# Gates of two branches by seven block products ahead of attention, and low halves of weight blocks on POOL

## The chip, the cores and the metric

The kernel runs on one core of a Trainium2 chip, as one launch. The metric is the device time in microseconds (us), from runs without the profiler; a profile comes from one execution more, and its span runs from the first to the last instruction. The engines are named as in the profile: PE (TensorE, matmuls), PEld (its weight loads), DVE (VectorE), ACT (ScalarE), POOL (GpSimd) and SP (SyncE, which issues the DMAs here).

## The reference

Two layers work on x, 512 tokens of 1024 channels, in float32. Three token mixers take their inputs from one projection of x; each is projected to 1024 channels, weighted by a sigmoid gate of its own, summed, and projected once more. A gated FFN of width 2816 follows.

```python
for l in range(DEPTH):
    proj = jnp.einsum('bsd,de->bse', x, w_in[l])
    (na_q, na_k, na_v, df_q, df_k, df_v, m_cq, m_ckv, m_kr, gate_pre) = jnp.split(proj, split_points, axis=-1)
    na_out = neighbourhood_attention(...)   # 8 heads of 64
    df_out = diff_attention(...)            # 4 heads, two softmaxes each
    mla_out = latent_attention(...)         # 8 heads, low-rank q and kv
    gates = jax.nn.sigmoid((gate_pre + b_gate[l]).astype(jnp.float32)).astype(x.dtype)
    gates = gates.reshape(b, s, N_BRANCH, D_MODEL)
    merged = (gates[:, :, 0] * jnp.einsum('bse,ed->bsd', na_out, w_branch[l, 0])
              + gates[:, :, 1] * jnp.einsum('bse,ed->bsd', df_out, w_branch[l, 1])
              + gates[:, :, 2] * jnp.einsum('bse,ed->bsd', mla_out, w_branch[l, 2]))
    mix = jnp.einsum('bsd,de->bse', merged, w_out[l])
    x = layer_norm(DN_ALPHA * x + mix, ln1_g[l], ln1_b[l])
    gu = jnp.einsum('bsd,df->bsf', x, w_ffn_in[l])
    hidden = jax.nn.silu(gu[..., :D_FF]) * gu[..., D_FF:]
    x = layer_norm(DN_ALPHA * x + jnp.einsum('bsf,fd->bsd', hidden, w_ffn_out[l]), ln2_g[l], ln2_b[l])
```

In differential attention a head's two probability matrices are combined, multiplied with the values, normalised by their root mean square, and scaled.

## The kernel before

**Float32 by halves.** Each float32 operand is split into a high half (a copy by ACT into the type fp32r) and a low half (the difference, by DVE). A product is three matmuls (`mm3`): high by high, high by low, low by high. x is held transposed as `xth` and `xtl`, channels on the partitions. Weights come by DMA in blocks of 128x1024 into `raw` (two buffers) and are split by `wsplit` into `whi` and `wlo` (four buffers each, lines 138 and 139).

**A layer.** First `na_values` projects the values of neighbourhood attention, token tile by token tile, while the layer norm of the layer before still delivers x. `latents` projects the low-rank inputs of latent attention in two column halves of 336. Then come four pairs of neighbourhood heads, four pairs of latent heads and four heads of differential attention, a last list, the output projection, and the FFN.

**Filler.** Attention's chains (scores, maximum, exponential, transposes, split, values) leave gaps on PE. `PLAN` is a table of thirteen lists: what is emitted after each of the four pairs, four pairs and four heads, and at the end. `G20h` means the gate of branch 2 for the first 256 of its 1024 columns (the second digit counts these steps): eight k tiles, two column blocks of 128, 48 matmuls of 512 tokens, then a Tanh (line 672); "h" says where the result lies. `M20` is the merge: a projection of a branch by `w_branch`, gated and added. Branch 0 is neighbourhood, 1 differential, 2 latent attention. Gates depend only on x and the weights, so they can stand anywhere after x; merges need their branch's attention, and those of branch 1 all four heads of the differential attention (though their first k tiles need only the first heads). A scheduler with a timeline of its own orders each engine's instructions when the kernel is built, by their emission and priorities; on the chip each engine runs its list in that order and waits where an operand is missing.

**A differential head** is `df_proj` (projection, rotation, transposes of q and k, their halves; the low half of k is copied to the other 64 partitions by DMA, in `stacks_k`), then `df_head` with four passes, one for each 128 queries: two score banks (lines 476, 477), two maxima (478) and exponentials (479), reciprocal, factor and combination (481 to 483), four transposes (486), the split `PP` (221, 222), four pairs of value matmuls (491, 492), and the scaling and normalisation of the result (494, 495, 497, POOL's 231 and 232, 499). After four passes the result is transposed (503) and split with a scale (224, 225).

**Seven block products.** In the FFN all but the first two sets of columns use `ffn_fast`: two weight column blocks (gate and up) by two halves of the tokens would be eight block products of 512 channels; with sums of weight blocks and sums of x (`x_sums`, formed once per layer after the second set, 26 DVE operations) seven do. Each `product` is 24 matmuls of 256 tokens (line 784).

Of the kernel before, what the change touches and what calls it, by code (L numbers as in the profile page):

```python
# [9 lines left out]
F32 = mybir.dt.float32  # L10
# [25 lines left out]
PLAN = [i.split() for i in (  # L36
    "G20h",
    "",
# [6 lines left out]
    "G03h M03",  # L45
    "",
    "M20 G21g G22h M21 M22",
# [29 lines left out]
def f32(ap):  # L77
    return ap.bitcast(F32)
# [3 lines left out]
def trunk(ctx, tc, x, ln_in, w_in, feat, bias, lamv, w_mla, w_mlr, w_mlv, w_branch, w_out,  # L82
# [22 lines left out]
    expo = cp.tile([128, 2], F32, name="expo")  # L105
    xd = [xs.tile([128, D], F32, name=f"xd{t}") for t in range(NT)]

    def bank(tag):
# [13 lines left out]

    def wload(segs, nk, ncol, now=True):
        raw = wp.tile([128, 1024], F32, tag="raw", name="raw", bufs=2)
        rv = raw[:, :nk * ncol].rearrange("p (k c) -> p k c", k=nk)
        c = 0
        for src in segs:
            w = src.shape[1]
            nc.sync.dma_start(rv[:, :, c:c + w], src.rearrange("(k p) c -> p k c", p=128))
            c += w  # L130
        hi, lo = wsplit(raw, nk * ncol, now)
        return hi.rearrange("p (k c) -> p k c", k=nk), lo.rearrange("p (k c) -> p k c", k=nk)

    def wsplit(raw, n, now=True):
        hi = wp.tile([128, 1024], F32R, tag="whi", name="whi")
        lo = wp.tile([128, 1024], F32R, tag="wlo", name="wlo")
        with tc.high_priority() if now else ExitStack():
            A.activation(hi[:, :n], raw[:, :n], AF.Copy)  # L138
            V.tensor_sub(lo[:, :n], raw[:, :n], f32(hi[:, :n]))  # L139
        return hi[:, :n], lo[:, :n]  # L140
# [5 lines left out]

    def wload_ks(src_of, widths, steps, now=True):

        res, k = [], 0
        for n in steps:  # L150
            res.append((k, n, wload(src_of(k * 128, (k + n) * 128), n, widths, now)))
            k += n
        return res
# [201 lines left out]
    def na_pair(l, p, vals):  # L355
        src = lambda a, b: [w_in[l, a:b, C_NQ + p * 128:C_NQ + (p + 1) * 128],
                            w_in[l, a:b, C_NK + p * 128:C_NK + (p + 1) * 128]]
        ch = wload_ks(src, 256, (4, 4))
        pq, pk = bank("acc"), bank("acc")
# [72 lines left out]
    def df_values(l, g):  # L432

        c = slice(C_DV + g * 256, C_DV + (g + 1) * 256)
        ch = wload_ks(lambda a, b: [w_in[l, a:b, c]], 256, (4, 4))
        vals = []
        for t in range(NT):
            p = bank("acc")[:, :256]
            gemm_x(p, ch, slice(0, 256), XT, tsl(t), KD)
            v = R.get()  # L440
            vv = v.rearrange("p (h s d) -> p h s d", h=2, s=2)
            split(vv[:, :, 0], vv[:, :, 1], p.rearrange("p (h d) -> p h d", h=2))
            vals.append(v)
        return vals

    def df_proj(l, h):
        src = lambda a, b: [w_in[l, a:b, C_DQ + h * 128:C_DQ + (h + 1) * 128],
                            w_in[l, a:b, C_DK + h * 128:C_DK + (h + 1) * 128]]
        ch = wload_ks(src, 256, (4, 4))
        stg = H.get()  # L450
# [57 lines left out]

    def latents(l, g):
        lat = [H.get() for _ in range(NT)]  # L510
        krs = [i[:, 672:800] for i in lat]
        for i in krs:
            G.memset(i, 0.0)
        for hf in range(2):
# [3 lines left out]
            for t in range(NT):  # L518
                p = bank("acc")[:, :336]
                gemm_x(p, ch, slice(0, 336), XT, tsl(t), KD)  # L520
                A.activation(lat[t][:, hf * 336:(hf + 1) * 336], p, AF.Copy)
        for t in range(NT):
            for a, b in ((0, 384), (384, 640)):
# [140 lines left out]
    def gates(l, b, mp, bg, dst):  # L664

        gc = C_GATE + b * D + mp * 256
        ch = wload_ks(lambda a, e: [w_in[l, a:e, gc:gc + 256]], 256, (4, 4))
        for mi in range(2):
# [5 lines left out]
    def merge(l, b, mp, o, merged, gt, first, mg=None):  # L674

        act = tuple(KTiles([t[i] for t in o]) for i in range(2))
        ch = wload_ks(lambda a, e: [w_branch[l, b, a:e, mp * 256:(mp + 1) * 256]], 256, (4,))
        for mi in range(2):
# [143 lines left out]

    def ffn_fast(l, m, sums):


        def load(t, base, kh):
            c = slice(base + m * 128, base + (m + 2) * 128)
            nc.sync.dma_start(t.rearrange("p (k c) -> p k c", k=4),
                              w_ffn_in[l, kh * 512:(kh + 1) * 512, c].rearrange("(k p) c -> p k c", p=128))
            return t  # L830
# [3 lines left out]

        g0, u0, u1 = load(H.get(), 0, 0), load(H.get(), D_FF, 0), load(H.get(), D_FF, 1)
        s = H.get()
        g1 = load(wp.tile([128, 1024], F32, tag="raw", name="raw", bufs=2), 0, 1)
        px, py, pz = bank("sc"), bank("pv"), bank("sc")
        product(px, halved(g0), from_x(0, 0), True)
        p1 = ptile()  # L840
        A.activation(p1, px, AF.Copy)
        t1, t2, t3, t4 = sums
        with tc.high_priority():
# [18 lines left out]
        H.put(s, u0, g0, u1)  # L862
        res = [hidden(px, p1)]
        res.append(hidden(u2, u3))
        return res

# [23 lines left out]
    for l in range(DEPTH):  # L890
# [18 lines left out]
        vals = na_values(l, na_v, na_slots)  # L909
        tiles, cq, ckv, kr = latents(l, fp[:, 25:30])  # L910
        merged, held, outs = [], {}, [[], [], []]
        mg = [[], []]

        def fill(steps):

            for kind, b, mp, *place in steps:
                b, mp, place = int(b), int(mp), "".join(place)
                if kind == "G":
# [10 lines left out]
                    if b:  # L929
                        held[b, mp] = pool, slot, gt  # L930
                    gates(l, b, mp, bg, gt)
                elif b == 0:
# [164 lines left out]
```

## Time and profile before

| what | value |
|---|---|
| time, median of 3 runs | 1848.38 us (1847.4 to 1851.75) |
| time of the profiled execution | 1850.09 us |
| its span | 1847.0 us |
| PE busy | 1814.9 us, 11248 matmuls |
| DVE busy | 1309.9 us, 2204 instructions |
| ACT busy | 897.8 us, 1612 instructions |
| POOL busy | 90.1 us, 165 instructions |
| mean granted clock of PE | 0.998 |

A row of the timeline gives start and duration in us, engine, line, operation, output and inputs, partitions x elements; what stands in brackets is the idle time before it and what ended it. A row of the table of groups gives the count, the total busy time and the mean in ns of one, then the idle time before. A row of the table by stretches gives for each stretch of the span the busy time and the number of instructions of each engine, the granted clock of PE, and the share and rate of the DMA engines. Matmuls overlap in PE's pipeline: what one costs is the distance between the starts of two, not its duration.

### The profile page before, as it was taken

The page shows a single profiled execution, that of the slowest core. Times are in us where ns is not written, and L with a number is a line of the kernel's source. Part 1 is how long each engine was busy: PE and PEld are TensorE (multiplying, and loading weights), DVE is VectorE, ACT ScalarE, POOL GpSimd, SP SyncE. Part 2 cuts the span into 40 slices and gives each one's busy share as a digit, 9 for nine tenths or more (in the row PEclk, how much of TensorE's full clock was granted, in tenths as well). Part 3 has the DMA queues.
Part 4 walks back from the last instruction along what each step waited for, and adds up shares of the span by engine and source line. Part 5 has one row for each costly group of instructions (what it writes and reads, how often), then busy time and mean ns, then how long its engine had stood idle before and what let it go on. Part 6 is the DMA issues. An engine that isn't in the chain of part 4 may idle for free.

```text
span 1847.0 us, 28601 instructions
## 1 busy us (share of the span) xinstructions
PE 1814.9 (98%) x11248; PEld 1617.9 (88%) x11248; DVE 1309.9 (71%) x2204; ACT 897.8 (49%) x1612; POOL 90.1 (5%) x165
## 2 busy tenths in 40 slices
PE   7999999999999999999999999999999999999997
PEld 5988899988888999999789888999888799899996
DVE  6488887665568767777756888867655687676766
ACT  4567776555433433334336677755554234333331
POOL 4100000000001000000001000000000000000001
PEclk9999999999999999999999999999999999999999
DMA  7453232222262132323445332322233512323222
GB/s 258 116 164 95 89 94 75 83 78 86 85 201 81 58 114 81 117 89 103 151 123 170 112 98 87 92 63 87 75 98 103 182 58 94 113 92 108 93 98 80
DMA packets 167766, 195.86 MB, mean 106 GB/s; under 512 B 8529, under 2 KB 132689, under 8 KB 167633
## 3 DMA queue, kind: packets, MB, share of 16 engines
q1 hardware_dynamic: 167632, 194.05, 33.7%
q8 instruction: 88, 1.44, 0.3%
q14 instruction: 46, 0.37, 0.1%
HBM read 177.24 MB, written 9.44 MB: 101 GB/s over the span
## 4 chain that ended last, share of the span: by engine, by line
PE 89%; DVE 5%; DMA 3%; ACT 1%; issue 1%; SPq 0%; POOLq 0%; DVEq 0%; POOL 0%; ACTq 0%
PE acc L157 18%; PE acc L158 18%; PE acc L156 17%; PE sc L784 9%; PE pv L784 7%; DVE wlo L139 2%; PE tr L648 2%; PE sc L156 1%; DMA f<-in_w_ffn_in_dram 1%; PE sc L158 1%; PE sc L157 1%; PE pv L157 1%; PE pv L158 1%; PE pv L156 1%; PE pv L491 1%
## 5 line engine op out<-in xcount | busy, mean ns | idle before, releaser
L138 ACT ACTIVATE whi<-raw 128x1024 fp32r<-128x1024 f32 (+3 forms) x246 | 254.3, 1034 | 289.4 <-PE acc L157 54.1
L139 DVE TENSOR_TENSOR wlo<-raw,whi 128x1024 fp32r<-128x1024 f32 (+3 forms) x246 | 293.6, 1195 | 132.2 <-ACT whi L138 129.0
L156 PE MATMUL acc<-xth,whi 128*128 128x512 f32 x512 | 204.0, 399 | 0.3 <-ACT f L672 0.3
L158 PE MATMUL acc<-xth,wlo 128*128 128x512 f32 x512 | 202.7, 396 | 0.0
L157 PE MATMUL acc<-xtl,whi 128*128 128x512 f32 x512 | 202.6, 396 | 0.0
L138 ACT ACTIVATE whi<-f 128x1024 fp32r<-128x1024 f32 x90 | 94.6, 1057 | 182.4 <-PE acc L158 102.3
L157 PE MATMUL acc<-wlo,r 128*128 128x512 f32 (+1 forms) x440 | 171.3, 390 | 2.2 <-DVE wlo L139 2.2
L158 PE MATMUL acc<-whi,r 128*128 128x512 f32 (+1 forms) x440 | 170.7, 389 | 0.0
L156 PE MATMUL acc<-whi,r 128*128 128x512 f32 (+1 forms) x440 | 169.0, 390 | 0.6 <-ACT whi L138 0.5
L157 PE MATMUL acc<-wlo,xth 128*128 128x256 f32 (+2 forms) x544 | 162.4, 299 | 1.3 <-DVE wlo L139 1.3
L156 PE MATMUL acc<-whi,xth 128*128 128x256 f32 (+2 forms) x544 | 161.7, 299 | 1.7 <-ACT whi L138 1.6
L158 PE MATMUL acc<-whi,xtl 128*128 128x256 f32 (+2 forms) x544 | 162.2, 299 | 0.0
L784 PE MATMUL pv<-r,whi 128*128 128x256 f32 x864 | 156.0, 280 | 2.3 <-DVE P L853 2.0
L784 PEld LDWEIGHTS pv<-r,whi 128*128 128x128 f32 x864 | 132.3, 188 | 5.2 <-issue 2.8
L139 DVE TENSOR_TENSOR wlo<-f,whi 128x1024 fp32r<-128x1024 f32 x90 | 109.4, 1221 | 34.7 <-ACT whi L138 34.7
L784 PE MATMUL sc<-xth,whi 128*128 128x256 f32 x432 | 120.5, 279 | 0.0
L784 PE MATMUL pv<-r,wlo 128*128 128x256 f32 x432 | 120.5, 279 | 0.0
L784 PE MATMUL sc<-xtl,whi 128*128 128x256 f32 x432 | 120.3, 279 | 0.0
L784 PE MATMUL sc<-xth,wlo 128*128 128x256 f32 x432 | 119.9, 279 | 0.0
L156 PEld LDWEIGHTS acc<-xth,whi 128*128 128x128 f32 x512 | 96.3, 188 | 19.5 <-ACT f L672 0.7
L157 PEld LDWEIGHTS acc<-xtl,whi 128*128 128x128 f32 x512 | 96.4, 188 | 18.8
L158 PEld LDWEIGHTS acc<-xth,wlo 128*128 128x128 f32 x512 | 96.4, 188 | 18.7
(255 smaller groups left out, 4462.2 us busy)
## 6 DMA issues: line engine op xcount, KB each, us to landing
raw<-in_w_in_dram SPq DMA_DIRECT2D x64, 512.0 KB, 3.7
f<-in_w_ffn_in_dram SPq DMA_DIRECT2D x54, 512.0 KB, 3.7
raw<-in_w_ffn_out_dram SPq DMA_DIRECT2D x44, 512.0 KB, 3.7
raw<-in_w_ffn_in_dram SPq DMA_DIRECT2D x34, 512.0 KB, 3.5
raw<-in_w_in_dram SPq DMA_DIRECT2D x64, 256.0 KB, 3.3
raw<-in_w_branch_dram SPq DMA_DIRECT2D x24, 512.0 KB, 3.3
raw<-in_w_out_dram SPq DMA_DIRECT2D x16, 512.0 KB, 3.6
r<-r SPq DMA_DIRECT2D x56, 128.0 KB, 2.7
```

The lines of the kernel that those rows point to most:

```text
L138: A.activation(hi[:, :n], raw[:, :n], AF.Copy)
L139: V.tensor_sub(lo[:, :n], raw[:, :n], f32(hi[:, :n]))
L156: T.matmul(o, lh[0], rh[0], start=first, stop=False)
L157: T.matmul(o, lh[0], rh[1], start=False, stop=False)
L158: T.matmul(o, lh[1], rh[0], start=False, stop=last)
L491: T.matmul(po[:, 0:256], ch_[:, tsl(k)], v, start=k == 0, stop=False)
L648: T.transpose(pt[:, tsl(i)], prs[i % 2][:, tsl(kp + i // 2)], ident)
L784: T.matmul(o[:, c], w[a][:, j, f], x[e], start=fresh and mi == 0 and j == 0 and n == 0, stop=j == 3 and n == 2, skip_group_check=True)
```

## The change

Two parts. The gates of branches 1 and 2 (eight steps of 256 columns per layer) are no longer formed by plain products as filler. `gates_fast` forms two steps at once by the seven block products that the FFN had; their code is now `block_set`, used by both. A layer has four such sets, and they are emitted around the two halves of the latents (two for branch 2 ahead of and between the halves, two for branch 1 behind them), all behind `x_sums`, which is now formed in attention too. Their Tanh runs on quarters of 256 tokens, and the results are stored to DRAM tiles `gd`; where `PLAN` has the G step of branch 1 or 2, only a load from there is left. `G20h` is moved from the first list to the tenth.

The second part: in attention's plain blocks (`na_pair`, `df_values`, `df_proj`, the gates of branch 0 and the merges, 40 blocks per layer) the low half is formed on POOL, in two operations of 512 columns, in place of one of 1024 on DVE.

```diff
@@ PLAN
-    "G20h",
+    "",
@@
-    "",
+    "G20h",
     "M20 G21g G22h M21 M22",
@@ trunk
+    gd = {(b, mp): xs.tile([128, 1024], F32, name=f"gd{b}{mp}") for b in (1, 2) for mp in range(4)}
@@ wsplit
         with tc.high_priority() if now else ExitStack():
             A.activation(hi[:, :n], raw[:, :n], AF.Copy)
-            V.tensor_sub(lo[:, :n], raw[:, :n], f32(hi[:, :n]))
+            if pool:
+                for a in range(0, n, 512):
+                    c = slice(a, min(a + 512, n))
+                    G.tensor_tensor(lo[:, c], raw[:, c], f32(hi[:, c]), op=OP.subtract)
+            else:
+                V.tensor_sub(lo[:, :n], raw[:, :n], f32(hi[:, :n]))
@@ na_pair, df_values, df_proj, gates, merge
-        ch = wload_ks(src, 256, (4, 4))
+        ch = wload_ks(src, 256, (4, 4), pool=True)
@@ latents
-    def latents(l, g):
+    def latent_rows(l, between):
         lat = [H.get() for _ in range(NT)]
-        krs = [i[:, 672:800] for i in lat]
-        for i in krs:
-            G.memset(i, 0.0)
+        between(0)
         for hf in range(2):
...
                 A.activation(lat[t][:, hf * 336:(hf + 1) * 336], p, AF.Copy)
+            between(1 + hf)
+        between(3)
+        return lat
@@ ffn_fast
-    def ffn_fast(l, m, sums):
+    def block_set(wsrc, top, bottom, sums):
...
-        res = [hidden(px, p1)]
-        res.append(hidden(u2, u3))
-        return res
+        return (px, p1), (u2, u3)
+
+    def ffn_fast(l, m, sums):
+        return [hidden(*i) for i in block_set(w_ffn_in[l], m * 128, D_FF + m * 128, sums)]
+
+    def gates_fast(l, b, mp, bg, sums):
+
+        col = C_GATE + b * D + mp * 256
+        for th, blocks in enumerate(block_set(w_in[l], col, col + 256, sums)):
+            for i, blk in enumerate(blocks):
+                t = ptile() if th == 0 and i == 0 else blk
+                for mi in range(2):
+                    m = b * 8 + 2 * (mp + i) + mi
+                    c = slice(mi * 256, mi * 256 + 256)
+                    A.activation(t[:, c], blk[:, c], AF.Tanh, bias=bg[:, m:m + 1], scale=0.5)
+                dst = gd[b, mp + i].rearrange("p (m t) -> p m t", m=2)
+                nc.sync.dma_start(dst[:, :, th * 256:th * 256 + 256], t.rearrange("p (m t) -> p m t", m=2))
@@ layer
-        tiles, cq, ckv, kr = latents(l, fp[:, 25:30])
+        sums = x_sums()
+        lat = latent_rows(l, lambda i: gates_fast(l, 2 - i // 2, i % 2 * 2, bg, sums))
...
+        tiles, cq, ckv, kr = latents(l, fp[:, 25:30], lat)
@@ fill
-                    gates(l, b, mp, bg, gt)
+                        for i in range(2):
+                            nc.sync.dma_start(gt[i], gd[b, mp][:, i * 512:(i + 1) * 512])
+                    else:
+                        gates(l, b, mp, bg, gt)
```

Before, PE's rows in the last head of differential attention of layer 0 mix the head's score, transpose (`tr`) and value (`pv`) matmuls with gate matmuls (`acc`, from `xth`):

```order
L476 MATMUL sc<-r_82,r_101 128x512
L477 MATMUL sc<-r_83,r_101 128x512
L156 MATMUL acc<-xth,whi 128x512
L491 MATMUL pv<-r_92,PP 128x256
L157 MATMUL acc<-xtl,whi 128x512
L158 MATMUL acc<-xth,wlo 128x512
L486 MATMUL tr<-cons,P 128x128 x3
L492 MATMUL pv<-r_92,PP 128x128
```

In the changed kernel the same head has on PE, from its third pass's scores on (482 and 483 are now the scores, 492 the transposes, 497 and 498 the values):

```order
L482 MATMUL sc<-r_82,r_89 128x512
L483 MATMUL sc<-r_83,r_89 128x512
L482 MATMUL sc<-r_98,r_88 128x512
L483 MATMUL sc<-r_99,r_88 128x512
L492 MATMUL tr<-cons,P 128x128 x4
L497 MATMUL pv<-r_108,PP 128x256
L498 MATMUL pv<-r_108,PP 128x128
L497 MATMUL pv<-r_109,PP 128x256
```

The gate matmuls between the head's own rows are gone. The place ahead of it, between head 2's last value matmul and head 3's first scores, reads on PE after the change (465 and 468 transpose q and k of head 3, 509 the result of head 2, `acc` is a merge's part):

```order
L498 MATMUL pv<-r_101,PP 128x128
L465 MATMUL tr<-cons,f_112 128x128 x4
L509 MATMUL tr<-cons,ost 128x128 x2
L468 MATMUL tr<-cons,f_112 128x128 x4
L162 MATMUL acc<-r_92,whi 128x512 x2
L163 MATMUL acc<-r_93,whi 128x512
L164 MATMUL acc<-r_92,wlo 128x512
L163 MATMUL acc<-r_93,whi 128x512
L164 MATMUL acc<-r_92,wlo 128x512
L482 MATMUL sc<-r_98,r_88 128x512
```

Ten transposes and six merge matmuls stand there, and the keys' transposes (468) stand behind the result's (509). At the start of layer 0, DVE had between the split of the values (`r` from `acc`) and the low halves of the latents' weights:

```order
L222 TENSOR_TENSOR r_78<-acc,r_78 128x2x128
L222 TENSOR_TENSOR r_79<-acc,r_79 128x2x128
L139 TENSOR_TENSOR wlo<-raw,whi 128x1008 x2
L222 TENSOR_TENSOR r_80<-acc,r_80 128x2x128
L139 TENSOR_TENSOR wlo<-raw,whi 128x672
```

and has after the change, in part (766 to 778 are `x_sums`, 857 to 859 sums of weight blocks, 145 a low half):

```order
L228 TENSOR_TENSOR r_89<-gt,r_88 128x512
L857 TENSOR_TENSOR f_117<-f_115,f_116 128x1024
L774 TENSOR_TENSOR xs<-xs,xtl 128x512
L777 TENSOR_TENSOR gt<-gt,xtl 128x512
L145 TENSOR_TENSOR wlo<-f_114,whi 128x1024
L228 TENSOR_TENSOR r_79<-acc,r_79 128x2x128
L766 TENSOR_TENSOR gt<-xth 128x512
L858 TENSOR_TENSOR f_115<-f_114,f_115 128x1024
L228 TENSOR_TENSOR r_93<-xs,r_92 128x512
L228 TENSOR_TENSOR r_80<-acc,r_80 128x2x128
L228 TENSOR_TENSOR r_95<-gt,r_94 128x512
L859 TENSOR_TENSOR f_114<-f_117,f_114 128x1024
```

The sums of x and of the first set's weights now stand among the values' splits, ahead of the latents' low halves.

More of the change, by code (lines that the diff above doesn't have):

```diff
@@ L120, in ptile, with wload @@
         return dp.tile([128, 512], F32, tag="P", name="P", bufs=4)
-    def wload(segs, nk, ncol, now=True):
+    def wload(segs, nk, ncol, now=True, pool=False):
         raw = wp.tile([128, 1024], F32, tag="raw", name="raw", bufs=2)
@@ L130, in wload, with wsplit @@
             c += w
-        hi, lo = wsplit(raw, nk * ncol, now)
+        hi, lo = wsplit(raw, nk * ncol, now, pool)
         return hi.rearrange("p (k c) -> p k c", k=nk), lo.rearrange("p (k c) -> p k c", k=nk)
-    def wsplit(raw, n, now=True):
+    def wsplit(raw, n, now=True, pool=False):
         hi = wp.tile([128, 1024], F32R, tag="whi", name="whi")
@@ L145, in wload_flat, with wload_ks @@
         return wsplit(raw, n)
-    def wload_ks(src_of, widths, steps, now=True):
+    def wload_ks(src_of, widths, steps, now=True, pool=False):
         res, k = [], 0
         for n in steps:
-            res.append((k, n, wload(src_of(k * 128, (k + n) * 128), n, widths, now)))
+            res.append((k, n, wload(src_of(k * 128, (k + n) * 128), n, widths, now, pool)))
             k += n
@@ L434, in df_values @@
         c = slice(C_DV + g * 256, C_DV + (g + 1) * 256)
-        ch = wload_ks(lambda a, b: [w_in[l, a:b, c]], 256, (4, 4))
+        ch = wload_ks(lambda a, b: [w_in[l, a:b, c]], 256, (4, 4), pool=True)
         vals = []
@@ L448, in df_proj @@
                             w_in[l, a:b, C_DK + h * 128:C_DK + (h + 1) * 128]]
-        ch = wload_ks(src, 256, (4, 4))
+        ch = wload_ks(src, 256, (4, 4), pool=True)
         stg = H.get()
@@ L521, in latents @@
                 A.activation(lat[t][:, hf * 336:(hf + 1) * 336], p, AF.Copy)
+            between(1 + hf)
+        between(3)
+        return lat
+    def latents(l, g, lat):
+        krs = [i[:, 672:800] for i in lat]
+        for i in krs:
+            G.memset(i, 0.0)
         for t in range(NT):
@@ L666, in gates @@
         gc = C_GATE + b * D + mp * 256
-        ch = wload_ks(lambda a, e: [w_in[l, a:e, gc:gc + 256]], 256, (4, 4))
+        ch = wload_ks(lambda a, e: [w_in[l, a:e, gc:gc + 256]], 256, (4, 4), pool=True)
         for mi in range(2):
@@ L676, in merge @@
         act = tuple(KTiles([t[i] for t in o]) for i in range(2))
-        ch = wload_ks(lambda a, e: [w_branch[l, b, a:e, mp * 256:(mp + 1) * 256]], 256, (4,))
+        ch = wload_ks(lambda a, e: [w_branch[l, b, a:e, mp * 256:(mp + 1) * 256]], 256, (4,), pool=True)
         for mi in range(2):
@@ L821, in ffn_plain, with load @@
         return res
-    def ffn_fast(l, m, sums):
-        def load(t, base, kh):
-            c = slice(base + m * 128, base + (m + 2) * 128)
+    def block_set(wsrc, top, bottom, sums):
+        t1, t2, t3, t4 = sums
+        def load(t, col, kh):
             nc.sync.dma_start(t.rearrange("p (k c) -> p k c", k=4),
-                              w_ffn_in[l, kh * 512:(kh + 1) * 512, c].rearrange("(k p) c -> p k c", p=128))
+                              wsrc[kh * 512:(kh + 1) * 512, col:col + 256].rearrange("(k p) c -> p k c", p=128))
             return t
@@ L833, in halved @@
             return wsplit(t, 1024)
-        g0, u0, u1 = load(H.get(), 0, 0), load(H.get(), D_FF, 0), load(H.get(), D_FF, 1)
+        g0, u0, u1 = load(H.get(), top, 0), load(H.get(), bottom, 0), load(H.get(), bottom, 1)
         s = H.get()
-        g1 = load(wp.tile([128, 1024], F32, tag="raw", name="raw", bufs=2), 0, 1)
+        g1 = load(wp.tile([128, 1024], F32, tag="raw", name="raw", bufs=2), top, 1)
         px, py, pz = bank("sc"), bank("pv"), bank("sc")
@@ L841, in ffn_fast @@
         A.activation(p1, px, AF.Copy)
-        t1, t2, t3, t4 = sums
         with tc.high_priority():
@@ L909, in trunk @@
         vals = na_values(l, na_v, na_slots)
-        tiles, cq, ckv, kr = latents(l, fp[:, 25:30])
+        sums = x_sums()
+        lat = latent_rows(l, lambda i: gates_fast(l, 2 - i // 2, i % 2 * 2, bg, sums))
+        for t in sums:
+            for hl in t:
+                R.put(*hl)
+        tiles, cq, ckv, kr = latents(l, fp[:, 25:30], lat)
         merged, held, outs = [], {}, [[], [], []]
```

## The prediction

> **What bounds the kernel now.** I read the page's busy times and chain first, then the table by stretches of 25 us, then the timeline of single stages.
>
> ```profile
> span 1847.0 us, 28601 instructions
> ...
> PE 1814.9 (98%) x11248; PEld 1617.9 (88%) x11248; DVE 1309.9 (71%) x2204; ACT 897.8 (49%) x1612; POOL 90.1 (5%) x165
> ...
> PE 89%; DVE 5%; DMA 3%; ACT 1%; issue 1%; SPq 0%; POOLq 0%; DVEq 0%; POOL 0%; ACTq 0%
> ```
>
> TensorE (PE) is busy nearly throughout, and 89% of the chain that ends last is its own matmuls. Only 32.1 us of the span (1847.0 - 1814.9) lie idle on it. So time can be won only by fewer matmul columns, and can be lost wherever PE begins to wait. VectorE (DVE) comes second, and the table by stretches shows where it is close behind:
>
> ```profile
> core 0: us, PE busy (x) PEld busy (x) DVE busy (x) ACT busy (x) POOL busy (x), PEclk, DMA share, GB/s
> ...
> 25.00:50.00 25.00, 24.40 (x126) 20.44 (x125) 11.63 (x17) 9.29 (x17) 5.08 (x4) 1.00 0.74 217
> ...
> 450.00:475.00 25.00, 25.00 (x119) 20.60 (x118) 15.82 (x26) 13.24 (x24) 0.00 (x0) 1.00 0.32 96
> 1300.00:1325.00 25.00, 25.00 (x120) 20.74 (x119) 15.21 (x23) 12.81 (x22) 1.58 (x4) 1.00 0.37 103
> ...
> 725.00:750.00 25.00, 24.53 (x209) 24.36 (x208) 22.44 (x25) 11.65 (x14) 0.00 (x0) 1.00 0.38 125
> ```
>
> 25 to 50 is the values' projection and the latents. 450 to 475 and 1300 to 1325 are the last heads of differential attention in layers 0 and 1: PE never waits there, because gate matmuls stand between the heads' own rows. 725 to 750 is a block set of the FFN with the sums of x: DVE is at 22.44 of 25, and PE just begins to wait. The changed kernel takes the filler out of the first kind of stretch and puts block sets where the values are.
>
> **What the block products save.** A matmul's own duration is a latency; what counts is the distance of starts.
>
> ```profile
> 442.02 0.39 PE L158 MATMUL acc<-xth,wlo 128*128 128x512 f32 x1
> 442.25 0.39 PE L156 MATMUL acc<-xth,whi 128*128 128x512 f32 x1
> ```
> ```profile
> 699.23 0.28 PE L784 MATMUL sc<-xth,whi 128*128 128x256 f32 x1
> ...
> 700.18 0.28 PE L784 MATMUL sc<-xth,wlo 128*128 128x256 f32 x1
> ```
>
> A gate matmul of 512 columns takes 0.230 us; eight steps of 256 columns take 0.95, so 0.118 each. Two plain gate steps are 96 matmuls, 96 x 0.230 = 22.1 us. The set that replaces them is 7 products x 24 = 168 matmuls, 168 x 0.118 = 19.8. One set saves 2.3, the eight sets of both layers **18 us** (22 if columns alone counted: 6 x 0.46 each). I take 18.
>
> **Where the filler was.** Gates of branches 1 and 2 leave the last two heads. By the order, from the second score of head 2 to the first open merge, PE then has only eight passes (scores, transposes, values) and scraps. A pass holds four 512-column matmuls (0.92), four transposes (0.36) and four value pairs (0.92): 2.2 us. Eight passes 17.6, less 6 matmuls ahead of the stretch (1.4), plus four more groups of transposes (1.4) and 12 merge matmuls (2.8): **20.4 us of PE work per layer**. Against it stands the chain of each pass and head:
>
> ```profile
> 466.76 0.60 PE L486 MATMUL tr<-cons,P 128*128 128x128 f32 x4
> 467.12 0.48 PE L156 MATMUL acc<-xth,whi 128*128 128x512 f32 x1
> ...
> 481.09 0.33 PE L491 MATMUL pv<-r,PP 128*128 128x256 f32 x1
> ...
> 481.32 0.34 PE L491 MATMUL pv<-r,PP 128*128 128x256 f32 x1
> 481.50 0.22 PE L492 MATMUL pv<-r,PP 128*128 128x128 f32 x1
> ```
> ```profile
> 480.83 0.17 DVE L481 RECIPROCAL ring<-ring 128x2 f32<-128x2 f32 x1 [0.84 <-ACT P L479]
> 481.04 0.22 DVE L482 SCALAR_TENSOR_TENSOR ring<-ring,lam 128x1 f32<-128x1 f32 x1
> 481.29 0.75 DVE L483 SCALAR_TENSOR_TENSOR P<-P,ring 128x512 f32<-128x512 f32 x1
> 481.96 0.68 DVE L222 TENSOR_TENSOR PP<-tr,PP 128x512 fp32r<-128x512 f32 x1
> 482.56 0.34 DVE L495 SCALAR_TENSOR_TENSOR ost<-pv,ring,otmp 128x128 f32<-128x128 f32 x1
> 484.33 0.29 DVE L499 TENSOR_SCALAR ost<-ost,ring 128x128 f32<-128x128 f32 x1 [1.43 <-POOL ring L232]
> ```
> ```profile
> L478 DVE TENSOR_REDUCE ring<-sc 128x1 f32<-128x512 f32 x64 | 44.0, 687 | 20.8 <-PE sc L477 20.6
> L225 DVE SCALAR_TENSOR_TENSOR r<-tr,fp,r 128x512 fp32r<-128x512 f32 x18 | 13.2, 749 | 15.2 <-ACT r L224 15.2
> L224 ACT ACTIVATE r<-tr,fp 128x512 fp32r<-128x512 f32 x18 | 11.9, 687 | 8.7 <-PE tr L503 7.7 <-PE tr L541 0.9
> L316 ACT ACTIVATE r<-tr 64x512 fp32r<-64x512 f32 x16 | 9.4, 591 | 4.3 <-PE tr L462 4.0
> L318 DVE TENSOR_TENSOR r<-tr,r 64x512 fp32r<-64x512 f32 x16 | 11.0, 688 | 12.0 <-ACT r L317 11.9
> ```
> ```profile
> r<-r SPq DMA_DIRECT2D x56, 128.0 KB, 2.7
> ```
>
> DVE owes each pass two reductions (2 x 0.687), the six operations of the timeline (0.17, 0.22, 0.75, 0.68, 0.34, 0.29): 3.8 us. Eight passes less the two reductions ahead are 29.2 (8 x 3.82 - 1.37). Operations overlap at their ends (0.75 long, the next starts 0.67 later), so 0.9 of it: 26 us. Between the heads lies a link that nothing covers. Head 2's last value matmul ends at 481.7 in the trace's like pass, its scaled result at 484.6 (2.9). Then come two groups of transposes in PE's order (0.7), ScalarE's (ACT) copies (0.69 and two of 0.59: 1.9), the low half of the keys (0.69) and their copy by DMA (2.7), before head 3's first score: 8.9, say **9 us**. Head 3's first exponential, as wide as the 0.69 copy, holds DVE up about 2 more (itself, its accumulator, PE's next rows), the last operations of both heads' pipelines leave DVE idle about 1.5 each, and head 3's end costs 2.9 + 0.4 + 0.69 + 0.75 = 4.7 until the merges of branch 1 open. Sum 26 + 9 + 2 + 3 + 4.7 = 45, less PE's 20.4: a stall of **25 us per layer, 50 in all**. The ends of this term: if only DVE's work counts (29.2, with 4 of the link's operations, x 0.9 = 30), the stall is 10 per layer; with no overlap and the link whole it is 33.
>
> **The sums ahead of the sets.**
>
> ```profile
> 34.44 0.69 DVE L222 TENSOR_TENSOR xtl<-tr,xth 128x512 fp32r<-128x512 f32 x1 [2.59 <-ACT xth L221]
> ...
> 41.55 0.32 PE L156 MATMUL acc<-whi,xth 128*128 128x336 f32 x1
> ```
> ```profile
> L754 DVE TENSOR_TENSOR gt<-xth x4: 681/684/685, 589.6 to 1509.6; 128x512 f32<-128x512 f32 x4
> ...
> L139 DVE TENSOR_TENSOR wlo<-raw,whi 128x1024 fp32r<-128x1024 f32 x220 | 269.6, 1226 | 104.4 <-ACT whi L138 101.3 <-PE tr L541 1.7
> ```
>
> The first row is one line of the FFN's `x_sums` (x4; least, median and most ns). Nine such lines twice per layer, and eight low halves, are 26 operations x 0.69 = 17.9 us of DVE; three sums of weights (two operands of 1024 columns, as the low half has) and three low halves, 6 x 1.22 = 7.3, follow before the second product. x is complete at 35.1 and PE's values end at 41.5: 6.4 us of PE work and the first product (24 x 0.118 = 2.8) stand beside what is then left of these 25 us. The order starts the sums on the earlier tiles, so about 17 us are left: a stall of 8 in layer 0. In layer 1 the values are spread more, and I take 4. Together **12, between 0 and 20**. Later sets need 16 us of DVE per 20 us of PE, beside latents that leave DVE free: hidden, as in the FFN. The tanh runs on ACT, 16 stores and 16 loads more on SP's queue move 0.5 MB each set, far ahead of their merges: nothing. If that cover went, a merge would wait a few us once.
>
> **Low halves on POOL.** 80 blocks move from DVE. Price, from the only large elementwise work POOL does:
>
> ```profile
> 24.08 3.51 POOL L248 TENSOR_TENSOR f<-f,f 128x512 f32<-128x512 f32 x2
> ...
> 24.31 2.14 DVE L139 TENSOR_TENSOR wlo<-raw,whi 128x1024 fp32r<-128x1024 f32 x1
> ```
> ```profile
> L138 ACT ACTIVATE whi<-raw 128x1024 fp32r<-128x1024 f32 x220 | 232.7, 1058 | 272.8 <-PE acc L157 52.5 <-DVE raw L857 46.3 <-DMA raw<-in_w_ffn_out_dram 45.8
> ```
>
> Two halves of 512 take up to 3.5 us on POOL, one block 1.23 on DVE by the row above: 2.3 later per block. The splits mostly wait for PE to free a buffer, so they run a block or more ahead (a block is 4 k of a gate, 5.5 us of PE), and I cost the move at 0. Without this cover it would be up to 80 x 2.3 = 184; it would show in attention's first projections, where PE has other rows, so I bound it at 6, and by -6 for the DVE time it frees near the heads.
> Beside POOL's operation a DVE block took 2.14 instead of 1.23. The Trainium skill, GPSIMD Engine Reference, section "Key points", says the two share their SBUF interfaces and contend when DVE has two SBUF inputs; the trace agrees. By that rule 80 blocks could slow some DVE operations by 0.9 each, at most 70 us of DVE time, hidden as long as PE has work.
> Two small stalls are left. The neighbourhood phase loses one gate step as filler; merges of branch 1 and the output projection now follow head 3 with no gates between. Each 0 to 5 per layer, taken 1.5: **6 in all**.
>
> **Sum.** 1850.1 - 18 + 50 + 12 + 6 = 1900 for the profiled execution, whose time (1850.09) lies 1.7 above the runs' median 1848.38: **1898**.
>
> **Rivals.**
> 1. *DVE alone limits the tails* (not slower). PE's queue lets head 3's projection, rope and scores slip under head 2, so the link is hidden; the sums begin early enough. Then 1848.4 - 18 (or 22) + 20 = 1846 to 1850, and 1840 where the starts close up from 0.9 to 0.8 of the operations' sum (27 per layer against 20.4). For it: DVE has 9 us free in 25 in the rows at 450. Against: the order puts no other PE row between head 2's last value matmul and head 3's first score than transposes and six merge matmuls. It decides where all stalls together stay under 18.
> 2. *The link half hidden*: tails of 15 each, sums 6: 1848.4 - 18 + 30 + 6 + 4 = 1870.
> 3. *PE's clock falls in the tails.* Early rows show matmuls 0.42 apart where warm ones are 0.23, and the last stretch, half idle, has a granted clock of 0.86:
>
> ```profile
> 15.10 0.63 PE L158 MATMUL acc<-whi,xtl 128*128 128x512 f32 x1
> 15.52 0.63 PE L156 MATMUL acc<-whi,xth 128*128 128x512 f32 x1
> ```
> ```profile
> 1825.00:1847.00 22.00, 12.69 (x55) 9.90 (x53) 18.00 (x31) 0.00 (x0) 4.99 (x8) 0.86 0.25 95
> ```
>
> At 0.42 the 20.4 us of a tail become 37; about half of these 17 lies in the chain (transposes, values), so 8 per layer: 1914. The Trainium skill (TensorE: Matmul & The Clock Gate, "HAM oscillation") has PE's clock halved after idle gaps over about 3.4 us; the link would be such a gap.
>
> **How the numbers follow.** A difference under 0.3% (5.5 us) can't be told from no change. Forecast (1878 to 1912) 0.61; rival 1 0.12 (faster 0.05, same 0.07); rival 2 (1855 to 1877) 0.13; rival 3, or POOL's blocks late (1912 to 1940), 0.14. All but rival 1 are slower: 0.88. The range 1862 to 1924 leaves out rival 1 (0.12), the low part of rival 2 (0.03) and the high half of rival 3 (0.05).
>
> **What would show it.** Right: stretches of 25 us at the end of differential attention with PE near half busy in both layers, a gap of about 9 us before head 3's first score whose releaser is the keys' DMA, PE waiting for DVE's sums before the second product, PE's matmul total about 18 us less. Wrong: PE busy as before in these stretches (rival 1), a granted clock well under 1 (rival 3), or waits of attention's matmuls for POOL's low halves. The prediction falls if the stall in the tails is under 10 us per layer.

## The result and the profile after

| | before | after |
|---|---|---|
| time, median | 1848.74 us (1847.4 to 1851.75, 4 runs) | 1955.15 us (1950.85 to 1960.07, 4 runs) |
| profiled execution, its span | 1850.09, 1847.0 us | 1960.07, 1958.3 us |
| ratio | | 1.0574, 95% interval 1.0545 to 1.0603 |

The changed kernel is 106 us slower; 50 were forecast, and the range ended at 1924. The page after, with the same three parts as the prediction's first fence:

```profile
span 1958.3 us, 30322 instructions
...
PE 1857.0 (95%) x11824; PEld 1664.2 (85%) x11824; DVE 1379.4 (70%) x2272; ACT 939.6 (48%) x1692; POOL 293.6 (15%) x325
...
PE 79%; DVE 10%; DMA 5%; ACT 4%; issue 2%; POOL 1%; SPq 0%; POOLq 0%; DVEq 0%; ACTq 0%
```

PE's idle time grew from 32 us to 101 (1958.3 - 1857.0), and its own share of the last chain fell from 89% to 79%. PE's busy time grew although it has less to do: overlapping latencies and slow matmuls count as busy. The table by stretches shows where (PE busy, PEld, DVE, ACT, POOL, granted clock, DMA):

```profile
25.00:50.00 25.00, 19.48 (x90) 15.46 (x89) 17.34 (x28) 7.91 (x16) 4.90 (x4) 0.91 0.62 182
50.00:75.00 25.00, 21.50 (x124) 20.04 (x124) 22.11 (x29) 11.74 (x16) 0.00 (x0) 0.75 0.39 106
225.00:250.00 25.00, 20.69 (x97) 17.08 (x96) 20.66 (x69) 16.86 (x45) 2.49 (x2) 0.80 0.32 94
450.00:475.00 25.00, 25.00 (x181) 23.29 (x180) 13.76 (x25) 13.95 (x28) 10.57 (x8) 1.00 0.33 94
525.00:550.00 25.00, 18.14 (x76) 12.88 (x75) 15.45 (x30) 13.09 (x33) 1.58 (x4) 0.73 0.11 32
1500.00:1525.00 25.00, 18.87 (x76) 13.61 (x74) 15.89 (x34) 13.17 (x36) 2.70 (x6) 0.74 0.11 32
```

Three places are new: the sums and first block set (25 to 75), neighbourhood attention (225 to 250) and the last differential heads (525 to 550, and 1500 to 1525 in layer 1). The middle of attention (450 to 475) is as full as it was. The clock is below 1 in each of the three.

To price the places, I took PE's rows in their order, each at its distance of starts (512 columns 0.2305 us, 336 0.155, 256 0.118, 128 0.062, a transpose 0.09), and set their running sum against the time at which marks of each stage stand in the trace. What the clock of the trace advances more than the sum is time that PE lost, by waiting or by slow matmuls. Worked out so, us lost per layer (mean of the two layers, each counted from its last transposes of x), with all of PE's work, in us, in the last column:

| kernel | start to neighbourhood's first score | neighbourhood | latent heads | differential heads | behind the heads, to the next norm's transposes | PE work, whole |
|---|---|---|---|---|---|---|
| before | 0.8 | 2.2 | 3.1 | 4.0 | 1.5 | 1782.6 |
| after | 17.9 | 18.2 | 2.1 | 31.3 | 6.9 | 1764.2 |
| difference | +17.1 | +16.0 | -1.0 | +27.3 | +5.4 | -18.4 |

64.8 lost per layer, 129.6 in both, less 18.4 of work, is 111.2; the spans differ by 111.3. So these five columns account for the change, and the experiments are read in them.

Part of these losses is slow matmuls. Where the trace's clock record stands at half, a matmul starts about twice its price after the one before (512 columns 0.43 us at 217 us, 0.23 elsewhere). So the price of the rows that start there is about the most that the clock itself cost: 4.9, 7.4, 0, 6.5 and 2.5 us per layer in the five columns, 21 of the 76. Before, no row of these columns stands at half.

First, what the three places look like. In layer 0's first block set, on DVE and PE:

```profile
43.85 1.23 DVE L857 TENSOR_TENSOR f<-f,f 128x1024 f32<-128x1024 f32 x1 [4.96 <-DMA f<-in_w_in_dram]
44.99 0.68 DVE L774 TENSOR_TENSOR xs<-xs,xtl 128x512 f32<-128x512 f32 x1
45.59 0.69 DVE L777 TENSOR_TENSOR gt<-gt,xtl 128x512 f32<-128x512 f32 x1
46.19 1.22 DVE L145 TENSOR_TENSOR wlo<-f,whi 128x1024 fp32r<-128x1024 f32 x1
```
```profile
42.45 0.27 PE L796 MATMUL sc<-xtl,whi 128*128 128x256 f32 x1
47.47 0.58 PE L796 MATMUL sc<-xth,wlo 128*128 128x256 f32 x1 [4.74 <-DVE wlo L145]
47.85 0.41 PE L796 MATMUL sc<-xth,whi 128*128 128x256 f32 x1
48.06 0.41 PE L796 MATMUL sc<-xtl,whi 128*128 128x256 f32 x1
```

These rows show a queue: a sum of weights waits 4.96 us on DVE for its DMA, two sums of x and the first product's low half stand behind it, and PE waits 4.74 us for that low half. Then the matmuls start 0.21 apart where 0.118 is normal. The Trainium skill (TensorE: Matmul & The Clock Gate, "HAM oscillation") says that an idle gap over about 3.4 us halves the clock for a while; this gap and these starts agree. Shorter waits were enough here too: behind one of 2.25 us, at 216 us, the granted clock is at half for 3.4 us.

In neighbourhood attention, two rotations on DVE beside POOL's low halves, in the changed kernel; then the same operations before; then what PE waits for from 200 to 250 us (total us, times, longest):

```profile
202.53 2.74 POOL L143 TENSOR_TENSOR wlo<-raw,whi 128x512 fp32r<-128x512 f32 x2 [6.77 <-ACT P L392]
```
```profile
202.89 1.23 DVE L433 TENSOR_TENSOR P<-f,cons 128x256 f32<-128x256 f32 x1
204.04 1.38 DVE L434 TENSOR_TENSOR P<-f,cons 128x128 f32<-128x128 f32 x1
205.34 0.28 DVE L435 TENSOR_TENSOR P<-f,cons 128x128 f32<-128x128 f32 x1
205.54 0.68 DVE L228 TENSOR_TENSOR PP<-tr,PP 128x512 fp32r<-128x512 f32 x1
```
```profile
107.42 0.42 DVE L427 TENSOR_TENSOR P<-f,cons 128x256 f32<-128x256 f32 x1
107.76 0.28 DVE L428 TENSOR_TENSOR P<-f,cons 128x128 f32<-128x128 f32 x1
```
```profile
PE tr L401 <- DVE P L397: 4.2, 3, 3.4
PE sc L385 <- DVE o L416: 2.3, 1, 2.3
```

An operation of 0.28 us takes 1.38, one of 0.42 takes 1.23, while POOL works; the next, after POOL has ended, is back at 0.28. PE waits for DVE's probabilities and outputs; in the whole profile no wait of it is put down to POOL's low halves. The longest of these waits, and the same pair of operations without POOL 3 us earlier:

```profile
226.39 0.60 DVE L397 TENSOR_SCALAR P<-P,ring 128x256 f32<-128x256 f32 x2
228.18 2.49 POOL L143 TENSOR_TENSOR wlo<-raw,whi 128x512 fp32r<-128x512 f32 x2 [3.57 <-ACT whi L139]
229.38 1.70 DVE L397 TENSOR_SCALAR P<-P,ring 128x256 f32<-128x256 f32 x2
230.96 1.09 PE L401 MATMUL tr<-cons,P 128*128 128x128 f32 x4 [3.36 <-DVE P L397]
```

POOL lengthens the pair by 1.1 us; the rest of the 3.36 is the chain itself (maximum, exponential), with no other matmul beside it. From 229.65 us the granted clock is at half for 10.2 us.

In the last head of layer 0, the link:

```profile
527.83 0.23 PE L498 MATMUL pv<-r,PP 128*128 128x128 f32 x1
...
530.85 0.48 PE L509 MATMUL tr<-cons,ost 128*128 128x128 f32 x1 [2.24 <-DVE ost L505]
531.97 1.09 PE L468 MATMUL tr<-cons,f 128*128 128x128 f32 x4 [0.65 <-DVE r L312]
...
535.42 0.63 PE L482 MATMUL sc<-r,r 128*128 128x512 f32 x1
536.29 0.74 PE L482 MATMUL sc<-r,r 128*128 128x512 f32 x1 [0.24 <-ACT r L323]
537.35 0.47 PE L483 MATMUL sc<-r,r 128*128 128x512 f32 x1 [0.32 <-DMA r<-r]
539.29 0.47 PE L483 MATMUL sc<-r,r 128*128 128x512 f32 x1 [1.47 <-DMA r<-r]
```

From the start of head 2's last value matmul to head 3's first score lie 7.6 us, to the score's low half, which waits for the keys' DMA, 9.5. It is not one gap that the keys' DMA ends, as the prediction had it: ahead of the first score PE is idle for 2.24 and 0.65 us, for head 2's result and for the queries' low half, both on DVE, and runs transposes and merge matmuls for the rest, most of them at half clock. The keys' DMA ends two later waits, of 0.32 and 1.47 us.

### The profile page after: what moved, and what is told of

Read it like the earlier page. It is cut to its first block, busy times and chain, and to the rows that moved or that the text cites. A ratio compares the mean times of both kernels' runs of the same rounds, so it can differ in the third digit from the quotient of the medians.

```text
span 1958.3 us, 30322 instructions
## 1 busy us (share of the span) xinstructions
PE 1857.0 (95%) x11824; PEld 1664.2 (85%) x11824; DVE 1379.4 (70%) x2272; ACT 939.6 (48%) x1692; POOL 293.6 (15%) x325
## 4 chain that ended last, share of the span: by engine, by line
PE 79%; DVE 10%; DMA 5%; ACT 4%; issue 2%; POOL 1%; SPq 0%; POOLq 0%; DVEq 0%; ACTq 0%
PE sc L796 13%; PE acc L163 13%; PE acc L162 13%; PE acc L164 13%; PE pv L796 10%; DVE wlo L145 2%; PE tr L660 1%; DMA raw<-in_w_ffn_in_dram 1%; ACT whi L139 1%; DMA f<-in_w_in_dram 1%; PE sc L163 1%; PE sc L162 1%; PE sc L164 1%; PE pv L163 1%; PE pv L162 1%
## 5 line engine op out<-in xcount | busy, mean ns | idle before, releaser
L139 ACT ACTIVATE whi<-raw 128x1024 fp32r<-128x1024 f32 (+5 forms) x230 | 237.1, 1032 | 289.9 <-DVE raw L870 57.3
L143 POOL TENSOR_TENSOR wlo<-raw,whi 128x512 fp32r<-128x512 f32 x160 | 209.2, 1331 | 689.2 <-ACT whi L139 630.1
L796 PE MATMUL pv<-r,whi 128*128 128x256 f32 x1248 | 225.7, 280 | 4.9 <-ACT whi L139 1.9
L145 DVE TENSOR_TENSOR wlo<-raw,whi 128x1024 fp32r<-128x1024 f32 (+4 forms) x150 | 176.7, 1178 | 55.6 <-ACT whi L139 55.2
L796 PEld LDWEIGHTS pv<-r,whi 128*128 128x128 f32 x1248 | 191.7, 188 | 8.5 <-ACT whi L139 2.6
L796 PE MATMUL sc<-xth,whi 128*128 128x256 f32 x624 | 176.4, 283 | 1.3 <-ACT whi L139 1.1
L796 PEld LDWEIGHTS sc<-xth,wlo 128*128 128x128 f32 x624 | 119.0, 191 | 6.8 <-DVE wlo L145 6.1
L796 PEld LDWEIGHTS sc<-xth,whi 128*128 128x128 f32 x624 | 119.2, 191 | 3.2 <-ACT whi L139 1.8
L796 PEld LDWEIGHTS sc<-xtl,whi 128*128 128x128 f32 x624 | 118.9, 191 | 1.5
L796 PEld LDWEIGHTS pv<-r,wlo 128*128 128x128 f32 x624 | 117.6, 188 | 0.0
```

What stands on the lines that cost most here:

```text
L143: G.tensor_tensor(lo[:, c], raw[:, c], f32(hi[:, c]), op=OP.subtract)
L796: T.matmul(o[:, c], w[a][:, j, f], x[e], start=fresh and mi == 0 and j == 0 and n == 0, stop=j == 3 and n == 2, skip_group_check=True)
```

## The experiments

Theory F (filler): PE loses time where gate matmuls stood beside attention's chains, and where the sums come ahead of the sets. Rival P: the losses come from POOL's low halves. The first four runs set them against each other.

**nopool**, the second part undone:

```diff
-        ch = wload_ks(src, 256, (4, 4), pool=True)
+        ch = wload_ks(src, 256, (4, 4), pool=False)
```
(and so in all five places)

> The changed kernel with the second part undone: all low halves on DVE again. Theory F (lost filler: PE stalls where the gate matmuls used to stand and where the sums wait on DVE): the loss stays, 1940 to 1960 us. Rival P (late low halves on POOL cause the loss in the neighbourhood phase, about 20 us per layer by the comparison of the two traces): 1910 to 1920 us, and the stretch of neighbourhood attention (184 to 270 us and 1150 to 1236 us) is back to about 76 us each, as before.

Measured: 1934.31 us, ratio 1.0463 (1.0445 to 1.0480). Lost per layer 17.4, 5.5, 3.7, 33.3, 4.1. Between the two: the neighbourhood phase gets back 12.7 of its 16.0 and the end 2.8; the latent and differential heads, where DVE has its blocks again, lose 3.6 more; the rest stays. The edit moves more than the engine: the scheduler ordered PE's rows anew, and the phase now holds 83.5 us of PE's work, 77.7 in the changed kernel. So 12.7 is what the part cost together with the order that came with it; no run holds the order fixed. With this open, P fits that phase and F the rest.

**poolonly**, the second part alone on the kernel before.

> The kernel before with the second part alone: the same 40 blocks per layer on POOL, gates plain. Theory F: PE has its filler, POOL's 2.5 us for a block hide behind it: 1845 to 1855 us. Rival P: the late low halves cost about 20 us per layer here too: 1875 to 1890 us.

Measured: 1852.04 us, ratio 1.0022 (1.0013 to 1.0031). The same POOL work, more of it (POOL also forms the low halves of the plain gates of branches 1 and 2 here), costs 4 us where PE has filler. So POOL's price is not its own: 21 us without cover, 4 with it.

**b1plain**, two sets per layer in place of four:

```diff
-        lat = latent_rows(l, lambda i: gates_fast(l, 2 - i // 2, i % 2 * 2, bg, sums))
+        lat = latent_rows(l, lambda i: gates_fast(l, 2, i, bg, sums) if i % 2 == 0 else None)
...
-                    if b:
+                    if b == 2:
```

> The changed kernel with branch 1's gates plain again, as filler in the last heads; only branch 2 by block products (two sets per layer in place of four). PE gets 9 us more matmul work. Theory F: the tails' stall (31 us in layer 0, 34 in layer 1 by the comparison of traces) goes almost whole: 1955 + 9 - 60 = about 1904, range 1890 to 1915. Rival (the tails are slow for another reason, the low halves on POOL or the loads of gates from DRAM): 1940 to 1965.

Measured: 1924.23 us, ratio 1.0416 (1.0401 to 1.0432): 31 us won where 51 were expected. The differential heads' loss fell from 31.3 to 12.5 per layer, but the 44 us of gates were used up ahead of head 3's end: from its first score on, 9 us stayed open. The other columns fell by 4 us per layer together.

**latfirst**, the sets behind the latents' halves:

```diff
-        between(0)
         for hf in range(2):
...
-            between(1 + hf)
-        between(3)
+            between(2 * hf)
+            between(2 * hf + 1)
```

> The changed kernel with the first two sets moved behind the first half of the latents, and the last two behind the second: 15 us of plain PE work then stand beside the 25 us of sums on DVE. If the stall of the first stage (15 us in layer 0, 12 in layer 1) is the wait for the sums: 1930 to 1940 us. Rival (the sets are slow in themselves there, or wait for their loads): 1950 to 1960 us.

Measured: 1935.38 us, ratio 1.0473 (1.0458 to 1.0489). The first column fell from 17.9 to 9.4 (20.9 to 14.8 in layer 0, 14.9 to 3.9 in layer 1). The same stretch as above, 50 to 75 us, now reads:

```profile
50.00:75.00 25.00, 24.23 (x168) 23.68 (x167) 21.04 (x27) 12.11 (x18) 0.00 (x0) 0.95 0.42 116
```

PE had 21.50 and a clock of 0.75 there. So half of that column's rise was the place of the sets. In layer 0 the queue itself stayed, and a wait moved with it:

```profile
44.04 1.23 DVE L856 TENSOR_TENSOR f<-f,f 128x1024 f32<-128x1024 f32 x1 [4.90 <-DMA f<-in_w_in_dram]
47.98 0.65 PE L162 MATMUL acc<-whi,xth 128*128 128x336 f32 x1 [6.20 <-DVE r L228]
```

The sum of weights still waits for its DMA, and a split of the values stands behind it, for which the latents' first matmul waits 6.20 us.

**g00first** and **late0** move filler and change neither work nor engines. g00first:

```diff
-    "",
+    "G00h",
     "",
     "",
-    "G00h",
+    "",
```

> The changed kernel with one gate step of branch 0 (11 us of PE work) moved in PLAN from behind the fourth neighbourhood pair to behind the first; low halves stay on POOL, PE's work stays the same. If the neighbourhood phase lost its time because POOL's late blocks have no filler beside them (the second part alone cost 4 us where the old filler stood): the phase's 16 us of loss per layer fall to about 5, 1930 to 1938 us. Rival (POOL's low halves are simply too late there, or slow DVE down): 1948 to 1958 us.

Measured: 1945.39 us, ratio 1.0532 (1.0516 to 1.0547), about half of the gain expected. First and second column fall (17.9 to 13.6, 18.2 to 13.9), the latent heads, from which the gate step came, rise from 2.1 to 6.3.

late0 moves three gate steps of branch 0, and the merges that need the last two, to later lists:

```diff
-    "G01h",
-    "M00",
-    "G02h",
-    "M01 M02",
-    "G03h M03",
-    "G20h",
-    "M20 G21g G22h M21 M22",
-    "G23h G10g M23",
+    "",
+    "M00",
+    "G01h",
+    "M01",
+    "",
+    "G20h M20 G02h",
+    "M02 G21g M21 G22h M22",
+    "G03h M03 G10g G23h M23",
```

> The changed kernel with branch 0's later gate steps and merges moved in PLAN from the latent heads to the differential heads: the same PE work, other places. By the order head 2 and the link to head 3 get filler, head 3 none. Theory F: about a third of the tails' stall (31 and 34 us) goes, so 10 per layer, and the latent heads, which had 2 us of loss, lose a few: 1935 to 1945 us. Rival (the tails are bound by DVE, whatever PE has beside them): 1950 to 1960 us.

Measured: 1958.58 us, ratio 1.0601 (1.0585 to 1.0617): no gain. The differential heads lose 27.9 in place of 31.3, the latent heads 7.4 in place of 2.1. There is not enough filler for all of attention; moved, it opens a gap where it came from.

**all3** (nopool, b1plain and latfirst at once) and **best1** (all four sets, nopool, latfirst, and filler moved as in g00first and late0).

> Three repairs at once on the changed kernel: low halves on DVE, branch 1's gates plain as filler, branch 2's two sets behind the halves of the latents. If the three losses are apart (21, 31 and 20 us by the single runs): 1883 us, range 1876 to 1890. If they share time: 1890 to 1905.

> All four sets kept (PE's 18 us saved), low halves on DVE, sets behind the latents' halves, and branch 0's gates and merges moved to where filler is short (one step to the neighbourhood phase, three to the differential heads). By the single runs 1955 - 21 - 20 - 15 = about 1900 us; below 1890 if the moves fit better together; above 1910 if the filler is then missing in the latent heads.

Measured: all3 1887.67 us, ratio 1.0225 (1.0208 to 1.0242): the three effects add up, within 5 us. best1 1932.91 us, ratio 1.0460 (1.0444 to 1.0475): 33 above what was expected; its losses (5.2, 14.1, 11.5, 26.2, 3.8) show the moved filler missing in the neighbourhood and latent phases, even with no low half on POOL.

**pooldummy** asks why POOL's part costs time: low halves on DVE, and behind each block

```diff
+            if dummy:
+                for a in range(0, n, 512):
+                    c = slice(a, min(a + 512, n))
+                    G.tensor_tensor(raw[:, c], raw[:, c], f32(hi[:, c]), op=OP.subtract)
```

> All low halves on DVE (as in the run nopool, 1934 us), and behind each of the same 40 blocks per layer POOL subtracts once more, from raw into raw, which nobody reads: POOL's load and its reads of SBUF are there, no matmul waits for its result. If POOL's 21 us come from DVE operations that it slows beside it: 1948 to 1958 us, and DVE operations with two SBUF inputs last longer beside POOL's. Rival (they come from low halves that arrive late): 1932 to 1938 us.

Measured: 1984.16 us, ratio 1.0729 (1.0712 to 1.0746), above both expectations: 50 us over nopool, though nothing reads what POOL writes. Neighbourhood loses 15.6 (nopool 5.5), the differential heads 43.9 (33.3). The neighbourhood phase holds nearly as much of PE's work here as in nopool (82.3 us, 83.5), so POOL's load costs time there also with that filler in place. It is not a clean measure of the changed kernel: DVE still forms its low halves here, `raw` is held longer, and the small operations of the heads' normalisation (lines 237, 238) stand in POOL's queue behind the dummies. Since PE has no wait for POOL's low halves in the changed kernel, their lateness is the weakest of the causes; how the 21 us divide between slowed DVE operations, this queue, the scheduler's order and the clock stays open.

**dfahead** takes the heads out of series:

```diff
+        nxt = df_proj(l, 0)
         for h in range(4):
-            qk = df_proj(l, h)
+            qk = nxt
...
+            if h < 3:
+                nxt = df_proj(l, h + 1)
             outs[1].append(df_head(h, qk, vals, lam, fp[:, 24:25]))
```

> The changed kernel with each differential head's projection, transposes and halves emitted ahead of the head before it: the link (result of head 2, keys' halves and their copy, before head 3's first score) goes, all else stays. If the link is 9 us of each tail: about 1955 - 2 x 9 = 1937 us, range 1930 to 1945. Rival (the passes themselves set the tail, by DVE's work and the chain of each): 1950 to 1957 us.

Measured: 1912.81 us, ratio 1.0352 (1.0323 to 1.0380): 42 us in place of 18. The differential heads' loss falls from 31.3 to 10.7 per layer. The stretch of the tail:

```profile
525.00:550.00 25.00, 20.54 (x89) 15.37 (x88) 17.62 (x36) 12.00 (x28) 3.40 (x8) 0.86 0.13 43
```

Head 3's first scores now stand beside head 2's passes, and its last score starts at 525.5 us (547.9 in the changed kernel). Not only the link went: the passes of two heads stand beside each other. And the granted clock, at half for 15 and 24 us of the differential heads in the changed kernel, does not fall in them here (the 0.86 lies behind them, from 536 us on), which is up to 6.5 of the 20.6 us.

**best2** (all3 and dfahead), **oneset** (one set per layer, G20, G21 and branch 1's gates plain, `G20h` back in the first list, low halves on DVE, the set behind the latents' first half):

> The run all3 (1888 us: low halves on DVE, only branch 2 by block products, its sets behind the latents' halves) with the heads' projections ahead as in dfahead. There gates fill the link already: 1880 to 1888 us. Below 1875 would say that the link still costs beside filler.

> One block set per layer (second half of branch 2), the other gates plain in the places of before, low halves on DVE, the set behind the latents' first half. PE is saved 4.6 us. Theory: each set takes 22 us of filler out of attention, whose own chains need about 370 us against 403 us of PE work before, so the first set costs little: 1848 - 5 + 0 to 10, so 1843 to 1853 us. Rival (every set costs its share, 10 us, from the first on, by the sums of x): 1855 to 1865 us.

Measured: best2 1861.55 us, ratio 1.0068 (1.0053 to 1.0083): 26 us less than all3, since all3 still lost 14.4 and 4.7 in the last two columns and best2 loses 4.1 and 1.4, as before the change. 1880 to 1888 was expected: beside half of the gates, the heads in series still cost time. oneset 1865.93 us, ratio 1.0093 (1.0077 to 1.0110): just above the rival's range; it loses 4.4 at the start (9.3 of it in layer 0), 7.9 in the heads and 5.0 behind them.

Three last runs. **dfbefore** is dfahead's edit on the kernel before; **best6** has four sets with all repairs; **best7** is oneset with the heads' projections ahead. In both the sums of x are emitted behind the latents' first half.

> The kernel before with the differential heads' projections emitted one head ahead, nothing else. If the order of the heads costs only where PE has no filler: within 0.3% of 1848 us. Rival (the heads in series cost time in any case): 1835 us or less, and dfahead's 42 us are then no measure of the tails.

> All four block sets per layer with all repairs: low halves on DVE, sets behind the latents' halves, the sums of x emitted behind the first half, projections one head ahead. By single effects 1955 - 21 - 20 - 42 = 1872 us if they are apart. PE has 9 us less work than in best2 (1862 us) and attention 40 us less filler: below 1862 would say that the block products pay once the waits are repaired, 1865 to 1885 that attention's own chains set the time.

> One block set per layer as in oneset (1866 us), with the projections one head ahead and the sums of x behind the first half of the latents. oneset lost about 6 us per layer behind the last head and 8 us in layer 0 ahead of the set: if the head order mends the first, 1852 to 1858 us; 1862 or more if not.

Measured: dfbefore 1847.01 us, ratio 0.9993 (0.9983 to 1.0002): the order of the heads costs nothing where PE has filler. best6 1873.80 us, ratio 1.0138 (1.0123 to 1.0153), 2 us from the sum of the single effects; it loses 34.1 per layer (7.7, 6.4, 3.7, 10.4, 5.9) against 11.6 before, more than the 9.2 per layer that it saves. best7 1849.85 us, ratio 1.0007 (0.9997 to 1.0016): level with before, its 4.6 us of saved work lost again, most of it ahead of layer 0's set (9.6 against 1.4).

No version was faster than the kernel before.

## Why the prediction was wrong

- **What the block products save: right.** 18 us forecast; PE's rows price at 18.4 less.
- **The last heads: right in place, and in size partly by luck.** 25 us per layer forecast; the column rose by 27.3. The loss lies in the last two heads (14 and 15 us per layer; the first two stay at about 1 each). The link was priced at 9 us; the trace has 7.6 to the first score and 9.5 to its low half. The term's upper end of 33 does not come out of its parts, which give 29.2 + 9 + 2 + 3 + 4.7 - 20.4 = 27.5. How the term is made up was off: up to 6.5 of it is the clock, which the sum left out; dfahead recovered 20.6 per layer, so the heads in series cost about twice the link; what is left, 10.7 - 4.0 = 6.7 over before, lies below the lower end of 10 that DVE's work alone was to give.
- **The sums ahead of the sets: a step that failed, in size and in the wait.** 12 us forecast in all, at most 20; 17.1 per layer measured in that column, 34. latfirst returned 20 us. The step counted DVE's work behind x but not what stands behind a waiting DVE instruction: the sum at 43.85 us waited 4.96 for its own DMA, with the first product's low half behind it, and PE then ran at about half speed. The prediction looked for the wait before the second product; it came in the first. Part of the column is not the sums: g00first, which puts a gate step between the latents and neighbourhood attention, took 4 us per layer off it.
- **Low halves on POOL at 0: the step that failed most.** It named its cover, that the splits run ahead of PE, and kept 6 us as a bound. Undoing this part returned 21 us (nopool). The neighbourhood phase lost 16 us per layer where 1.5 had been taken for the missing gate step; nopool, with its new order, returned 12.7 of it. The cover was misread: of the 272.8 us that ACT sat idle before the splits, the row puts 52.5 down to PE, 46.3 to DVE and 45.8 to DMA, so they did not mostly wait for PE. The price was looked for in late low halves: two of them took 2.66 us on POOL on the mean (2 x 1.331), not 3.5, and PE shows no wait for them; it waited for the DVE operations beside them. What covered the part was PE's filler: with it the same work cost 4 us (poolonly). The prediction had the row for it, a DVE block at 2.14 in place of 1.23 beside POOL, and the condition, that slowed DVE operations are hidden as long as PE has work; it did not put the two together in the phase from which the change takes the work.
- **The small stalls: too small.** Taken at 1.5 each per layer; the end behind head 3 rose by 5.4.
- **The rivals.** Not slower: refuted. The clock: it did fall (0.73 and 0.74 in the tails' stretches, 0.75 in the first set, 0.80 in neighbourhood attention), but not in the tails alone: priced at 8 us per layer there, it cost up to 6.5, and up to 14.8 more in the other columns, where rival 3 had none. It follows PE's gaps, so a repair that closes a gap returns its share too; no run takes the clock apart from them.

The forecast direction had most of the chance, and rightly. Neither failed step explains the miss alone: nopool (1934) and latfirst (1935) both lie above the range's 1924, and both repairs together would give 1955 - 21 - 20 = 1914, which no run has by itself. POOL's term was bounded against the kernel before, where filler stands everywhere, and the change takes that filler away; the sums' term left out a queue behind a DMA.

## What to carry to other kernels

Independent matmuls that a scheduler uses as filler can be worth more than their own time: making them cheaper and placing them elsewhere can expose the chains that they stood beside. Ask for each stage how long its chain takes without filler before pricing the saved columns, and count a cost as hidden only by work that is still there after the change. If filler must go, overlap the chains with each other first (here one head's projection ahead of the head before it, worth 42 us in the changed kernel and nothing in the kernel before).

## What was not expected of the hardware

While POOL ran a two-input operation of 512 columns, DVE operations with both operands in SBUF lasted up to five times as long (0.28 to 1.38 us for 128 columns, 0.42 to 1.23 for 256); those that read PSUM beside them kept their time. The table of groups of the changed kernel has both kinds (mean ns after the comma):

```profile
L484 DVE TENSOR_REDUCE ring<-sc 128x1 f32<-128x512 f32 x64 | 43.3, 686 | 25.5 <-PE sc L483 25.2
L489 DVE SCALAR_TENSOR_TENSOR P<-P,ring 128x512 f32<-128x512 f32 x32 | 28.8, 901 | 0.6
L501 DVE SCALAR_TENSOR_TENSOR ost<-pv,ring,otmp 128x128 f32<-128x128 f32 x32 | 11.1, 346 | 6.1 <-ACT otmp L500 6.1
```

The maximum (from `sc`) and the scaling (from `pv`) keep their 687 and 348 ns, also the 20 and 4 of them that overlap POOL's low halves (685 and 342); the combination (from two `P`) rose from 748 to 901: the 6 that overlap took 1572 on the mean, the other 26 the old 747. This is the rule of the Trainium skill's GPSIMD Engine Reference ("Key points") that the prediction cited, and the trace agrees; its size for short operations was the surprise.
